# A layer norm applied to rows between two sets of transposes, in place of statistics sent through DRAM

## The chip, the cores and the metric

The kernel runs on one core of a Trainium2 chip. The metric is the device time of one execution in microseconds; a profiled execution gives the traces. The engines are TensorE (PE; PEld is its weight load), VectorE (DVE), ScalarE (ACT), GpSimd (POOL) and SyncE (SP), whose queue issues nearly all transfers between DRAM and the on-chip memory.

## The reference

One layer of a streaming encoder, for 2048 prompt tokens and 32 sample tokens (with 1024 cached). A combined projection of the normed input feeds two groups. The convolution group, which the change touches, has 512 channels; the attention group has 8 heads with a compressed key/value latent.

```python
h = _rmsnorm(x, g_pre)
a, b, gate_c, q_c, kv_c, k_r, gate_a = jnp.split(h @ w_in, SPLITS, axis=-1)
glu = a * jax.nn.sigmoid(b)
y = depthwise_conv(concat(hist, glu), width 31) + conv_b          # 512 channels
y_conv = silu(_layernorm(y, ln_g, ln_b))                          # over the 512 channels of a token
...                                                               # attention gives y_att
mixed = concat(y_conv * silu(gate_c), y_att * silu(gate_a)) @ w_out
return x + _rmsnorm(mixed, g_post)
```

`_layernorm` takes mean and variance of each token over its 512 channels, subtracts, divides, then applies a gain and a bias for each channel.

## The kernel before, in words

The work runs in three stages. **Stage A** makes the projection in two halves of 1024 tokens (the second with the 32 sample tokens), with channels on the partitions and tokens in the columns: for each block of 128 channels, TensorE multiplies each of two or three token chunks by the weight, each product as three matmuls of a high and a low part (lines 359 to 361). `load_w` loads a block's weight (512 KB through SP into one raw buffer); ScalarE rounds it to the high part, GpSimd subtracts for the low part (`split`, lines 155 and 156). Tokens come in as rows, are normed, and turned by TensorE (`transpose_x`, lines 330 to 332: ScalarE makes `xh`, VectorE makes `xl`). The order within a half is a and b blocks (GLU), latents, then the gates; in half 0 the last two gate blocks (`lastpair`) run with the loading of half 1's tokens among them.

The convolution is **background work**: `later(f, cost)` puts closures into a queue, and `bg(n)`, called behind each chunk of matmuls, takes from it what `n` pays for. 31 taps for each of four channel blocks run on VectorE into PSUM (line 381) and on ScalarE and GpSimd into `acc` (lines 386 to 390). In half 0 the layer norm follows in the same queue. What `bg` puts out stands in program order; a scheduler at build time then orders each engine's instructions by a timeline that it simulates.

The layer norm of a tile of 128 tokens: `emit_ln` turns the four blocks of `acc` into a PSUM tile with tokens on the partitions (line 198); VectorE takes mean and variance of each row (lines 178 and 179); GpSimd makes the inverse root with an add and a power (lines 142 and 143); SP writes the 128 pairs to DRAM (`st_d`, line 185) and reads them back as a row that is broadcast to all partitions (`z`, line 187); two places later in the queue `emit_ln2` subtracts and multiplies `acc` by these rows on VectorE (line 193). When all tiles are done, `emit_mix` takes one channel block with all its 1024 tokens: it loads the gate (line 206), applies gain, bias and Silu on ScalarE (line 208), multiplies on GpSimd, stores to `mix_d` (line 210).

**Stage B** is the attention. Here the order of TensorE, ScalarE, VectorE and GpSimd is written by a planner in the kernel: streams of steps (`q`, `s`, `t`, `v`, `p`, `l`, `o`) and a list of loose steps (`after`) are put out in order of simulated times, with a price for each step (`hold`, `t_pe`, `t_act`, `t_dve`; a transfer counts `DL` = 10 us). Keys and values are made, copied by ScalarE into one of four staging buffers (`staged`, line 834; two of them are halves of the tile `lng`), stored to DRAM, and loaded again for each head. The layer norm of half 1's nine tiles is stream `l`, one tile for every `BI` = 4 steps: `l_run` turns, `stats` sends the statistics through DRAM, `norm` subtracts and multiplies on GpSimd 20 simulated us later and stores the rows unscaled to `mix_d` (line 1403). Gain, bias, Silu and gate for them follow in **stage C**, the output projection (`split_mix`, line 1683).

SP's queue issues in order: a transfer that waits for a semaphore holds those behind it.

## Time and profile before

| | |
|---|---|
| median of 3 runs | 1310.7 us (1310.13 to 1317.46) |
| the profiled execution | 1310.61 us, span 1308.8 us |
| TensorE busy | 1232.9 us, 94% of the span |
| VectorE, ScalarE, GpSimd busy | 883.0 (67%), 749.2 (57%), 627.2 us (48%) |
| mean granted clock of TensorE | 0.974 of full speed |

A row of a busy table gives for each engine the time in which it had work in that stretch. The granted clock is TensorE's, 1.00 at 2.4 GHz and 0.50 at 1.2 GHz; between them, both occurred. "Idle before" is the time an engine stood still just before the instructions of a group, with the instruction or transfer that ended it.

### The profile page before, as it was taken

The page shows a single profiled execution, that of the slowest core. Times are in us where ns is not written, and L with a number is a line of the kernel's source. Part 1 is how long each engine was busy: PE and PEld are TensorE (multiplying, and loading weights), DVE is VectorE, ACT ScalarE, POOL GpSimd, SP SyncE. Part 2 cuts the span into 40 slices and gives each one's busy share as a digit, 9 for nine tenths or more (in the row PEclk, how much of TensorE's full clock was granted, in tenths as well). Part 3 has the DMA queues.
Part 4 walks back from the last instruction along what each step waited for, and adds up shares of the span by engine and source line. Part 5 has one row for each costly group of instructions (what it writes and reads, how often), then busy time and mean ns, then how long its engine had stood idle before and what let it go on. Part 6 is the DMA issues. An engine that isn't in the chain of part 4 may idle for free.

```text
span 1308.8 us, 20918 instructions
## 1 busy us (share of the span) xinstructions
PE 1232.9 (94%) x7272; PEld 1100.1 (84%) x7272; DVE 883.0 (67%) x1814; ACT 749.2 (57%) x1748; POOL 627.2 (48%) x680
## 2 busy tenths in 40 slices
PE   7999999699999998868996999999999999999997
PEld 6889987589899997757896999999999998788876
DVE  4299898255997913646684888898988884543333
ACT  5366722155565223656685888888888884345221
POOL 5299942136999322545554434545554365111110
PEclk8999999899899999989998999999999999999999
DMA  8122253223313323596666323355245356944332
GB/s 294 31 72 80 79 140 105 56 57 109 113 49 87 113 83 91 107 117 123 115 76 92 37 44 43 76 58 63 46 79 47 39 90 132 284 156 144 95 109 69
DMA packets 166606, 124.23 MB, mean 95 GB/s; under 512 B 67031, under 2 KB 148489, under 8 KB 166499
## 3 DMA queue, kind: packets, MB, share of 16 engines
q1 hardware_dynamic: 166339, 122.82, 42.2%
q8 instruction: 57, 0.93, 0.4%
q14 instruction: 50, 0.41, 0.3%
q10 hardware_dynamic: 160, 0.07, 0.0%
HBM read 83.64 MB, written 39.21 MB: 94 GB/s over the span
## 4 chain that ended last, share of the span: by engine, by line
PE 71%; DMA 13%; DVE 6%; POOL 5%; ACT 3%; issue 2%; SPq 1%; POOLq 0%; DVEq 0%; ACTq 0%
PE mm L361 7%; PE mm L360 7%; PE mm L359 7%; PE sps L1117 4%; PE sps L1119 4%; PE sps L1118 4%; DMA st_d<-bmv 3%; PE ops L1255 2%; PE yx L1710 2%; PE yx L1711 2%; PE yx L1709 2%; DVE cv L381 2%; PE sps L1711 2%; PE sps L1710 2%; PE sps L1709 2%; PE mm L441 2%
## 5 line engine op out<-in xcount | busy, mean ns | idle before, releaser
L381 DVE SCALAR_TENSOR_TENSOR cv<-glu,cwT,cv 128x1024 f32<-128x1024 f32 x186 | 239.7, 1289 | 6.0
L1154 ACT ACTIVATE pc<-pc,row 128x512 f32<-128x512 f32 (+3 forms) x320 | 210.2, 659 | 34.3 <-DVE pc L1133 33.6
L360 PE MATMUL mm<-xl,wh 128*128 128x352 f32 (+1 forms) x584 | 209.2, 358 | 2.6 <-DVE xl L347 2.5
L361 PE MATMUL mm<-xh,wl 128*128 128x352 f32 (+1 forms) x584 | 208.0, 356 | 3.2 <-POOL wl L156 3.2
L359 PE MATMUL mm<-xh,wh 128*128 128x352 f32 (+1 forms) x584 | 208.0, 358 | 0.3 <-ACT xh L331 0.3
L1224 DVE TENSOR_TENSOR ptl<-tp,pth 128x512 fp32r<-128x512 f32 (+1 forms) x288 | 187.8, 656 | 28.9 <-ACT pth L1220 26.2
L1220 ACT CAST pth<-tp 128x512 fp32r<-128x512 f32 (+1 forms) x288 | 159.9, 558 | 35.0 <-PE tp L1208 24.7
L1133 DVE TENSOR_SCALAR_CACHE_REDUCE pc<-sps,row 128x512 f32<-128x512 f32 (+2 forms) x192 | 125.7, 655 | 21.8 <-PE sps L1119 14.6
L1117 PE MATMUL sps<-kh,qh 128*128 128x512 f32 (+3 forms) x320 | 132.8, 415 | 4.0 <-DVE pc L1133 2.6
L360 PEld LDWEIGHTS mm<-xl,wh 128*128 128x128 f32 x584 | 112.2, 192 | 13.8 <-DVE xl L347 3.9
L361 PEld LDWEIGHTS mm<-xh,wl 128*128 128x128 f32 x584 | 112.3, 192 | 13.3 <-POOL wl L156 3.5
L1119 PE MATMUL sps<-kh,ql 128*128 128x512 f32 (+3 forms) x320 | 116.7, 365 | 6.6 <-POOL ql L156 6.6
L359 PEld LDWEIGHTS mm<-xh,wh 128*128 128x128 f32 x584 | 112.4, 193 | 10.9 <-ACT xh L331 0.6
L149 POOL TENSOR_TENSOR acc<-acc,ptap 128x512 f32<-128x512 f32 x92 | 118.7, 1306 | 4.6 <-ACT acc L386 2.7
L1118 PE MATMUL sps<-kl,qh 128*128 128x512 f32 (+3 forms) x320 | 116.1, 363 | 0.0
L156 POOL TENSOR_TENSOR wl<-wraw,wh 128x1024 fp32r<-128x1024 f32 x27 | 64.9, 2403 | 97.6 <-ACT wh L155 97.5
L156 POOL TENSOR_TENSOR ql<-qf,qh 128x256 fp32r<-128x256 f32 x64 | 46.9, 735 | 114.0 <-ACT qh L155 98.8
L1255 PE MATMUL ops<-ptl,vb 128*128 128x256 f32 x288 | 85.9, 298 | 5.6 <-DVE rl L1163 4.4
L1253 PE MATMUL ops<-pth,vb 128*128 128x256 f32 x288 | 88.2, 306 | 2.2 <-ACT pth L1220 2.2
L149 POOL TENSOR_TENSOR yp<-yp,low 64x256 f32<-64x256 f32 x64 | 46.9, 734 | 89.2 <-ACT low L1264 88.1
L1133 DVE TENSOR_SCALAR_CACHE_REDUCE pc<-sps 128x512 f32<-128x512 f32 (+3 forms) x128 | 80.0, 628 | 12.8 <-PE sps L1119 11.2
L1202 PE MATMUL tp<-ident,pc 128*128 128x128 f32 x288 | 80.3, 279 | 6.6 <-ACT lng L834 4.9
(386 smaller groups left out, 3265.2 us busy)
## 6 DMA issues: line engine op xcount, KB each, us to landing
wraw<-in_w_in SPq DMA_DIRECT2D x31, 512.0 KB
xr<-in_x_prompt SPq DMA_DIRECT2D x16, 512.0 KB
out_y_p<-src SPq DMA_DIRECT2D x32, 256.0 KB
mix<-mix_d SPq DMA_DIRECT2D x7, 1024.0 KB
gate_d<-gt SPq DMA_DIRECT2D x24, 176.0 KB
xt<-in_x_prompt SPq DMA_DIRECT2D x8, 512.0 KB
gate_d<-gt SPq DMA_DIRECT2D x16, 256.0 KB
gat<-gate_d SPq DMA_DIRECT2D x32, 128.0 KB
```

The source lines that it names most:

```text
L149: nc.gpsimd.tensor_tensor(dst, x, y, op)
L359: nc.tensor.matmul(ps[:, :n], wh[:, k], rh, start=(k == 0), stop=False)
L360: nc.tensor.matmul(ps[:, :n], wh[:, k], rl, start=False, stop=False)
L361: nc.tensor.matmul(ps[:, :n], wl[:, k], rh, start=False, stop=(k == KT - 1))
L381: nc.vector.scalar_tensor_tensor(box["ps"], x, cw(j), box["ps"], ALU.mult, ALU.add)
L1117: nc.tensor.matmul(d, qh[:, qs], kh[b][:, ks], start=True, stop=False)
L1118: nc.tensor.matmul(d, qh[:, qs], kl[b][:, ks], start=False, stop=False)
L1119: nc.tensor.matmul(d, ql[:, qs], kh[b][:, ks], start=False, stop=True)
L1133: nc.vector.tensor_scalar(p_[:, :m], d, -SCALE, r["mx"][:, c - 1:c] if c else None, ALU.mult, ALU.min, accum_out=r["mx"][:, c:c + 1])
L1154: nc.scalar.activation(p_, p_, AF.Exp, bias=r["mx"][:, ns - 1:ns], scale=-1.0, accum_out=r["ls"][:, c:c + 1])
L1220: nc.scalar.copy(out=ph[:, :nn], in_=ps[:, :nn])
L1224: nc.vector.tensor_tensor(pl[:, :nn], ps[:, :nn], ph[:, :nn].bitcast(F32), ALU.subtract)
```

## The change

The statistics no longer go through DRAM. VectorE applies mean and inverse root to the turned rows, where they are one number for each partition, and writes the normed rows into the place in `acc` that the tile's channels had; a second set of four transposes turns them back into PSUM (`ln_back`). In half 0, `emit_ln2` then applies gain, bias and Silu from PSUM to `acc` (four instructions for each tile), multiplies by the gate and stores to `mix_d`, tile by tile. The gate of a tile is loaded by `emit_ln` into one of two slots of the tile `lng`, which is now allocated once. `emit_mix` goes. The layer norm is queued after the convolution gates are made, and `emit_ln2` of a tile is queued ahead of `emit_ln` of the tile two later. Half 1's x transposes of `lastpair` take PSUM from the pool `mm` (four buffers) in place of `tp` (two). In stage B, `l_run` is followed by `stats` (with the tensor_scalar), `back` (transposes, in a further PSUM slot) and `out` (a copy by ScalarE, then the store). Two hunks that only name `lng` directly are left out here.

```diff
--- before.py
+++ after.py
@@ -162,52 +162,54 @@
     acc = accp.tile([P, CT, HALF + DEC], F32, name="acc")
 
     ln_pool = {}
-    zs = {}
+    lng = lnp.tile([P, HALF + DEC], F32, name="lng", bufs=1)
+    gslot = [lng[:, i * 512:(i + 1) * 512].rearrange("p (k t) -> p k t", k=CT) for i in range(2)]
 
     def queue_ln(jobs):
         for i in range(len(jobs) + LL):
+            if i >= LL:
+                later(lambda a=jobs[i - LL]: emit_ln2(*a), LC)
             if i < len(jobs):
                 later(lambda a=jobs[i]: emit_ln(*a), LC)
-            if i >= LL:
-                later(lambda a=jobs[i - LL]: emit_ln2(*a), LC)
-
-    def ln_stats(t, ps, r):
+
+    def ln_turn(ps, c0, r):
+        for i in range(CT):
+            nc.tensor.transpose(ps[:r, i * P:(i + 1) * P], acc[:, i, c0:c0 + r], ident)
+
+    def ln_rows(ps, c0, r):
 
         st = small.tile([P, 6], F32, name="bst")
         mv = small.tile([P, 2], F32, name="bmv")
         nc.vector.bn_stats(st[:r], ps[:r])
         nc.vector.bn_aggr(mv[:r], st[:r])
         rsqrt_eps(mv[:r, 1:2], mv[:r, 1:2], 1)
-        return mv
-
-    def ln_spread(t, mv, r):
-        rows = st_d[t * P:t * P + r]
-        nc.sync.dma_start(out=rows, in_=mv[:r])
-        z = lnp.tile([P, P, 2], F32, name="z")
-        nc.sync.dma_start(out=z[:, :r], in_=rows.partition_broadcast(P))
-        return z
-
-    def ln_apply(z, c0, r, subtract, multiply):
-        x = acc[:, :, c0:c0 + r]
-        for tt, op, q in ((subtract, ALU.subtract, 0), (multiply, ALU.mult, 1)):
-            tt(x, x, z[:, :r, q].unsqueeze(1).broadcast_to([P, CT, r]), op)
+        x = ln_x(c0, r)
+        nc.vector.tensor_scalar(x, ps[:r].rearrange("p (k c) -> p k c", k=CT), mv[:r, 0:1], mv[:r, 1:2],
+                                ALU.subtract, ALU.mult)
+
+    def ln_x(c0, r):
+        c0 = c0 if r == P else 0
+        return acc[:r, :, c0:c0 + P]
+
+    def ln_back(ps, c0, r):
+        x = ln_x(c0, r)
+        for i in range(CT):
+            nc.tensor.transpose(ps[:, i * P:i * P + r], x[:, i], ident[:r, :r])
 
     def emit_ln(t, c0, r):
         ps = ln_pool["ps"].tile([P, 512], F32, name="tp")
+        ln_turn(ps, c0, r)
+        ln_rows(ps, c0, r)
+        nc.sync.dma_start(out=gslot[t % 2], in_=gate_d[0:CT, :, c0:c0 + r].rearrange("k p t -> p k t"))
+
+    def emit_ln2(t, c0, r):
+        ps = ln_pool["ps"].tile([P, 512], F32, name="tp")
+        ln_back(ps, c0, r)
+        y = acc[:, :, c0:c0 + r]
         for i in range(CT):
-            nc.tensor.transpose(ps[:r, i * P:(i + 1) * P], acc[:, i, c0:c0 + r], ident)
-        zs[t] = ln_spread(t, ln_stats(t, ps, r), r)
-
-    def emit_ln2(t, c0, r):
-        ln_apply(zs.pop(t), c0, r, nc.vector.tensor_tensor, nc.vector.tensor_tensor)
-
-    def emit_mix(i, t0, n):
-        g = lnp.tile([P, HALF + DEC], F32, name="lng", bufs=1)
-        nc.sync.dma_start(out=g[:, :n], in_=gate_d[i, :, t0:t0 + n])
-        y = acc[:, i, :n]
-        nc.scalar.activation(y, y, AF.Silu, bias=col(LN_B, i), scale=col(LN_G, i))
-        pool_tt(y, y, g[:, :n], ALU.mult)
-        nc.sync.dma_start(out=mix_d[i, :, t0:t0 + n], in_=y)
+            nc.scalar.activation(y[:, i], ps[:, i * P:i * P + r], AF.Silu, bias=col(LN_B, i), scale=col(LN_G, i))
+        pool_tt(y, y, gslot[t % 2], ALU.mult)
+        nc.sync.dma_start(out=mix_d[0:CT, :, c0:c0 + r].rearrange("k p t -> p k t"), in_=y)
 
     with ExitStack() as pa:
         tp = pa.enter_context(tc.tile_pool(name="tpa", bufs=2, space=PSUM))
@@ -583,8 +585,6 @@
                             load_lat(lat_todo.pop(0))
                     bg(BG[half] / len(chunks))
                 conv_taps(i, half)
-            if half == 0:
-                queue_ln([(j, j * P, P) for j in range(8)])
             latents(half, tiles)
             if half:
                 def new_conv(dst, src, off):
@@ -608,8 +608,7 @@
                     evac_gate(half, slot, c0, m, emit_chunk(wts[key], c0, m))
                     bg(BG[half] / len(chunks))
                 if half == 0 and n == CT - 1:
-                    for i in range(CT):
-                        later(lambda i=i: emit_mix(i, 0, HALF), LC)
+                    queue_ln([(j, j * P, P) for j in range(8)])
             if lastpair:
                 need(lastpair[1])
                 owed[0] = 0.0
@@ -625,7 +624,7 @@
                             stage_x([ahead.pop(0)], 0)
                         bg(2 * LC)
                     if ci == 0:
-                        transpose_x(range(8, 12), 0, fill=True)
+                        transpose_x(range(8, 12), 0, mm, fill=True)
                 flush()
             if half:
                 bg(1e6)
...
@@ -1369,43 +1367,46 @@
             prods.pop(0)[2][1](ready)
 
 
-        zslots = Slots(4)
-        zslots.free = [0.0, 4.0, 12.0, 14.0]
         lns = list(ln_jobs)
         n_ln, n_done = [0], [0]
 
         def l_ready():
             if not lns or turn_at[0] < BS + BI * n_ln[0]:
                 return None
-            return latest(tps.ready(), zslots.ready())
+            return tps.ready()
 
         def l_run(ready):
             t, c0, r = lns.pop(0)
             n_ln[0] += 1
             kslot = tps.take()
             ps = tp.tile([P, 512], F32, name="tp")
-            for i in range(CT):
-                nc.tensor.transpose(ps[:r, i * P:(i + 1) * P], acc[:, i, c0:c0 + r], ident)
+            ln_turn(ps, c0, r)
             te = hold("pe", t_pe(256, 4), ready)
-            zk = zslots.take()
 
             def stats(ready):
-                mv = ln_stats(t, ps, r)
-                te = hold("dve", t_dve(512) + 0.1, ready)
+                ln_rows(ps, c0, r)
+                te = hold("dve", t_dve(512) + 0.2, ready)
+                te = hold("pool", 0.3, te)
+                te = hold("dve", t_dve(512), te)
                 tps.give(kslot, te)
-                te = hold("pool", 0.3, te)
-                z = ln_spread(t, mv, r)
-
-                def norm(ready):
-                    ln_apply(z, c0, r, pool_tt, pool_tt)
-                    te = hold("pool", 2.4, ready)
-                    zslots.give(zk, te)
+                after("pe", PE_["l"], lambda: latest(te, tps.ready()), back)
+
+            def back(ready):
+                k = tps.take()
+                ps = tp.tile([P, 512], F32, name="tp")
+                ln_back(ps, c0, r)
+                te = hold("pe", t_pe(256, 4), ready)
+
+                def out(ready):
+                    nc.scalar.copy(out=acc[:, :, c0:c0 + r], in_=ps.rearrange("p (k t) -> p k t", k=CT)[:, :, 0:r])
+                    te = hold("act", t_act(512), ready)
+                    tps.give(k, te)
                     nc.sync.dma_start(out=mix_d[0:CT, :, HALF + c0:HALF + c0 + r].rearrange("k p t -> p k t"),
                                       in_=acc[:, :, c0:c0 + r])
                     n_done[0] += 1
                     if n_done[0] == len(ln_jobs):
                         done["mix"] = te
-                after("pool", PE_["ln"], te + 2 * DL, norm)
+                after("act", PE_["ln"], te, out)
             after("dve", PE_["ln"], te, stats)
 
         pinned = ExitStack()
```

## Rows read from the trace of the kernel before

**Rows 1.** The page: TensorE's busy tenths in 40 slices of the span.
```profile
PE   7999999699999998868996999999999999999997
```

**Rows 2.** Stretches: length, busy PE, PEld, DVE, ACT, POOL, clock, DMA, GB/s.
```profile
220.00:260.00 40.00, 28.29 (x113) 21.86 (x113) 11.17 (x20) 5.95 (x9) 7.69 (x12) 0.83 0.33 76
260.00:300.00 40.00, 36.39 (x235) 34.40 (x236) 19.38 (x39) 19.84 (x36) 13.23 (x17) 0.96 0.20 51
300.00:340.00 40.00, 36.14 (x209) 35.56 (x208) 30.08 (x25) 21.09 (x32) 32.29 (x23) 0.91 0.49 143
...
560.00:600.00 40.00, 29.26 (x168) 24.14 (x167) 20.09 (x56) 23.75 (x56) 16.59 (x28) 0.87 0.84 128
...
680.00:720.00 40.00, 29.41 (x191) 27.50 (x190) 22.87 (x70) 22.90 (x61) 15.82 (x17) 0.88 0.65 91
```

**Rows 3.** TensorE in order of time: start, duration, unit, line, operation.
```profile
223.40 0.63 PE L359 MATMUL mm<-xh,wh 128*128 128x512 f32 x1
223.82 0.63 PE L360 MATMUL mm<-xl,wh 128*128 128x512 f32 x1
...
226.62 0.60 PE L198 MATMUL tp<-ident,acc 128*128 128x128 f32 x4
226.98 0.47 PE L359 MATMUL mm<-xh,wh 128*128 128x512 f32 x1
227.29 0.39 PE L360 MATMUL mm<-xl,wh 128*128 128x512 f32 x1
227.52 0.39 PE L359 MATMUL mm<-xh,wh 128*128 128x512 f32 x1
```

**Rows 4.** Groups, TensorE, 216 to 348 us: busy, ns | idle before, releaser.
```profile
L361 PE MATMUL mm<-xh,wl 128*128 128x352 f32 x115 | 38.9, 340 | 3.2 <-POOL wl L156 3.2
...
L330 PE MATMUL tp<-ident,xt 128*128 128x128 f32 x32 | 5.5, 299 | 11.1 <-DVE xl L332 5.6 <-DVE bst L178 5.4
L198 PE MATMUL tp<-ident,acc 128*128 128x128 f32 x32 | 5.0, 274 | 1.9 <-DVE acc L408 1.9
```

**Rows 5.** Groups of the other engines in 216 to 348 us.
```profile
L193 DVE TENSOR_TENSOR acc<-acc,z 128x512 f32<-128x512 f32 x16 | 11.0, 690 | 42.0 <-DMA z<-st_d 41.9
...
L208 ACT ACTIVATE acc<-acc,cols 128x1024 f32<-128x1024 f32 x4 | 4.6, 1232 | 6.2 <-DVE acc L193 6.2
...
L484 ACT ACT_TABLE_LOAD x2 | 2.6, 1283 | 0.0
L346 ACT ACTIVATE xh<-mm,cols 128x32 fp32r<-128x32 f32 x8 | 2.3, 288 | 13.1 <-DVE xl L347 11.7 <-PE mm L343 1.4
...
L149 POOL TENSOR_TENSOR acc<-acc,lng 128x1024 f32<-128x1024 f32 x4 | 9.6, 2406 | 7.2 <-ACT acc L208 6.8 <-DMA lng<-gate_d 0.4
```

**Rows 6.** SP's waits, 216 to 345 us: total us, times, longest.
```profile
SPq L187 <- DMA st_d<-bmv: 28.5, 7, 6.7
SPq L210 <- POOL acc L149: 22.6, 4, 6.6
```

**Rows 7.** SP's waits, 505 to 720 us.
```profile
SPq L187 <- DMA st_d<-bmv: 45.1, 9, 8.1
```

**Rows 8.** SP's issues in order of time: start, us, line, transfer.
```profile
541.27 0.32 SPq L185 DMA_DIRECT2D st_d<-bmv  x1
...
552.00 0.32 SPq L187 DMA_DIRECT2D z<-st_d  x1
```

**Rows 9.** The chain of waits in 505 to 720 us: start, us, what.
```profile
555.08 14.73 DMA v_d<-lng
...
683.71 9.56 DMA gat<-gate_d
```

**Rows 10.** Groups of GpSimd in 505 to 720 us.
```profile
L149 POOL TENSOR_TENSOR acc<-acc,z 128x512 f32<-128x512 f32 x16 | 20.9, 1307 | 0.6
...
L143 POOL TENSOR_TENSOR bmv<-bmv,nhalf 128x1 f32<-128x1 f32 x8 | 4.6, 571 | 0.7
```

More of the change, by code (lines that the diff above doesn't have):

```diff
@@ L681, in load_wkv @@
         def load_wkv():
-            raw = lnp.tile([P, HALF + DEC], F32, name="lng", bufs=1)[:, 0:NH * P].rearrange("p (h c) -> p h c", h=NH)
+            raw = lng[:, 0:NH * P].rearrange("p (h c) -> p h c", h=NH)
             nc.sync.dma_start(out=raw, in_=w_kvb.rearrange("p (h c) -> p h c", h=NH))
@@ L821, in prep_tasks @@
                     (lambda: latest(box["t2"], tps.ready()), query(1))]
-        spare = lnp.tile([P, HALF + DEC], F32, name="lng", bufs=1)
         stgw = wk.tile([P, 1024], F32, name="stgw", bufs=1)
         stgs = [stgw[:, i * 512:(i + 1) * 512] for i in range(2)]
-        stgs += [spare[:, i * 512:(i + 1) * 512] for i in range(2)]
+        stgs += [lng[:, i * 512:(i + 1) * 512] for i in range(2)]
         stg = Slots(len(stgs))
```

## The prediction

> **What bounds the kernel now.** I read the summary first: of 40 slices of 32.7 us, TensorE is busy for nine tenths or more in all but the first and the last, one at 229 us and several between 490 and 720 us [rows 1], so a change can only pay where TensorE stands still, runs at its lower clock, or loses work. The table by stretches says how much that is [rows 2]. These are the two places of the layer norm: its first half is worked off in the background around the turn from half 0 to half 1, its second half inside the attention plan.
>
> In 220 to 340 us TensorE idles 11.7 + 3.6 + 3.9 = 19.2 us. The granted clock of 0.83, 0.96 and 0.91 means that 34%, 8% and 18% of these stretches ran at 1.2 instead of 2.4 GHz; weighted with the busy share that is 19 us of work. A 512-column matmul follows the one before it after 0.42 us at the lower clock and 0.23 us at the upper [rows 3], so 45% of 19 us, 8.6 us, is lost. Together **28 us are lost in this stretch**.
>
> What ends these waits? The transposes of x wait 11.1 us for VectorE (for the split of x and for the statistics), others 1.9 us for the last convolution tap, and one matmul 3.2 us for GpSimd's weight split [rows 4]. VectorE itself is not busy then: its 16 subtract and multiply instructions stood 41.9 us waiting for the broadcast statistics [rows 5]. The split and the statistics stood behind them in its queue, and TensorE behind those. The SP queue is held too: before each broadcast it waits until the write of the statistics has landed, 28.5 us in seven times [rows 6], and weight loads stand behind that. So the round trip through DRAM is on the path here.
>
> In the attention stage the same wait holds SP for 45.1 us in nine times [rows 7]. The two worst stretches lose 10.7 and 10.6 us idle [rows 2], and by the same sum as above 3.4 and 3.2 us to the clock: **28 us** in both. The first is tied to the round trip: SP issues a statistics write at 541.3 us and its broadcast only at 552.0 us [rows 8]; behind it go the stores of k and v, of which the one issued at 555.1 us takes 14.7 us, and ScalarE's next evacuation, then TensorE, wait for its staging buffer [rows 9]. In the second the chain runs through a gate load of 9.6 us [rows 9] for which GpSimd waits with the key split behind it; SP was late there for several reasons, one of them a broadcast.
>
> After 720 us nothing of the layer norm is left, so what TensorE gains or loses before is passed on to the end.
>
> **The change part by part: half 0.** It removes 8 statistics writes, 8 broadcasts and the 16 VectorE instructions (11.0 us of work, 41.9 us of waiting [rows 5]). It adds on VectorE 8 tensor_scalar of 512 columns out of PSUM, 8 x 0.69 = 5.5 us by the nearest row [rows 5]. They wait for GpSimd's add and power; the power takes 0.57 us [rows 10]. Behind that wait on VectorE stand the split of x and the next statistics, for about 1 us a tile, 8 us in place of 41.9.
>
> TensorE gets 8 x 4 transposes back. Four of them cost 0.36 + 0.31 - 0.23 = 0.44 us of its time [rows 3], so 3.5 us. They come two places of the background queue after the first four; in between a whole chunk of 24 matmuls, 5.6 us, runs, which covers the chain from statistics to tensor_scalar (about 3 us). If that cover were gone, 8 x 3 us would stand on TensorE.
>
> ScalarE's 4 Silu of 1024 columns (1.23 us) become 32 of 128 columns. Between 0.29 us for 32 columns and 1.23 us for 1024 [rows 5] a straight line gives an estimate of 0.38 us, 12.2 us for 4.9. The last five tiles fall among half 1's sigmoids; if each comes alone, I count 9 table loads where 3 are now, 6 x 1.28 = 7.7 us more [rows 5]. ScalarE is busy for 26 of 80 us in 220 to 300 us [rows 2], so I cost both at nothing; if all of the table loads stood before an evacuation that TensorE waits for, it would be 8 us.
>
> On this a rule of the Trainium skill speaks against the change. The loads here last 1.28 us, and the sigmoid starts right behind one. The page "ScalarE: Activation LUTs", section "What ACT_TABLE_LOAD costs", adds a drain of about 1.38 us to that, 2.66 us a switch, and asks that calls be batched by table set. By the page the six would cost ScalarE 16 us; the trace shows only the 1.28 us of it.
>
> GpSimd's gate multiplication goes from 4 x 2.41 = 9.6 us [rows 5] to 8 x 1.31 = 10.5 us [rows 10], but most of it moves ahead of 300 us, where it is 74% idle [rows 2], and out of 300 to 340 us, where it is busy for 32 of 40 us and delays the weight split that TensorE waits for (3.2 us [rows 4], and the lower clock after it). The x transposes move to the larger PSUM pool, so that they no longer share two buffers with the layer norm; that goes with the waits above. Half 1's convolution overwrites the accumulator and waits for the last tile's store, as it now waits for the four stores of channels.
>
> SP: 8 gate loads of 256 KB replace 4 of 512 KB, 8 stores replace 4. A gate load writes over the slot of two tiles before, so SP waits for that tile's multiplication first; the store of that tile waits for the same thing. The nearest row is the 22.6 us that SP waits for 4 multiplications before their stores [rows 6], 5.6 us each. Behind them stand the weight loads, of which the first two of half 1 have little slack. No row shows the new order; the bounds are 0 (the wait falls where nothing is due) and 5.6 us for each of 8 tiles; I take 5 us on TensorE for this and all other new waits, near the low end, since the multiplication is then no longer behind a broadcast.
>
> Sum of half 0: of 28 us, 4 us stay (the wait for the last tap with the lower clock after it), 3.5 us of transposes and 5 us of new waits are added: **15.5 us gained**, between 5 (new waits of 15 us) and 24 (none, and the transposes inside waits).
>
> **Half 1, in the attention plan.** 9 statistics writes and 9 broadcasts go, with SP's 45.1 us of waiting; GpSimd loses 20.9 us of work for the eight full tiles [rows 10]. TensorE gets 9 x 0.44 = 4 us, VectorE 9 x 0.69 = 6.2 us, ScalarE 9 copies of 512 columns, about half of a 1.23 us row, 5.5 us. VectorE's new wait for GpSimd is planned at 0.3 us where the power alone takes 0.57 [rows 10]; attention's score evacuations stand behind it, some 9 x 0.7 us on an engine that is half idle in these stretches [rows 2]. The plan's order changes too, as its costs do. Of the 14 us of the first stretch I take 8 as gained, because the stores stood directly behind the blocked queue; of the 14 us of the second a quarter, because SP had other waits there; the added 4 us on TensorE are paid in full. **7.5 us gained**, between 4 lost and 24 gained.
>
> **Sum.** The profiled execution took 1310.6 us (span 1308.8), the median of three is 1310.7, so the two are the same: 1310.6 - 15.5 - 7.5 = **1288 us**.
>
> **The rivals.** (a) *Only half 0 gains.* k and v still go through four staging buffers, and the stores themselves are slow (14.7 us [rows 9]); then the attention stage stands as before, with about 2 of its added 4 us on the path: 1310.6 - 15.5 + 2 = 1297 us. For it speaks that those stores are on the chain; against it, that they were issued late. (b) *ScalarE takes back half 0's gain.* Five blocks of two table loads and four Silu (2 x 1.28 + 4 x 0.38 = 4.1 us) stand between sigmoid evacuations, and the weight chain behind them slips by most of 2.6 us for each: 13 us back, half 0 keeps 2.5, attention gives 2: 1310.6 - 2.5 - 2 = 1306 us. Against it speaks ScalarE's idle time. By the skill's price of a switch (same page and section) it would be twice that. (c) *Slower: SP is held longer than now.* If the gate loads of six tiles and the stores of eight each hold SP 5.6 us, that is 79 us against 28.5 + 22.6 = 51 us now [rows 6]. At today's rate (28 us lost for 51 held) TensorE loses 43 us, 15 more than now, with the transposes 1310.6 + 15 + 3.5 + 4 = 1333 us without a gain in attention, 1322 with it; about 1326. It decides when the mean wait goes over 51 / 14 = 3.6 us. Against it: the order is load and store behind the same multiplication, so that the second finds it done. (d) *SP wholly freed.* Both stretches of the attention stage recover and half 0 gains its 21: 1310.6 - 20 - 20 = 1270 us.
>
> **How the numbers follow.** Forecast 0.45 (1278 to 1296), (a) 0.22, (b) 0.13, (c) 0.08, (d) 0.12. From 1268 to 1307 us some 8 in 10 lie: it takes in the forecast, (a), about half of (b), most of (d), and leaves (c) out. About 1% is what a measurement here can tell from no change; 1% faster is 1297.6 us. (a) straddles that: faster 0.45 + 0.12 + 0.12 = 0.69; same 0.10 + 0.13 = 0.23; slower 0.08.
>
> **What would show it.** In the changed kernel's table by stretches, 220 to 340 us should show TensorE idle under 8 us and half 1's work starting some 15 us sooner. VectorE's waits for a transfer should be gone from the list of waits, its wait for GpSimd's power at about 1 us a tile. SP's waits should show the multiplication in place of the statistics; over 3.6 us each would mean (c). Up to 9 table loads in half 1's first chunks, with TensorE waiting for evacuations, would mean (b). In the attention stage the k and v stores should be issued within 2 us of their copies; if the two stretches there still lose 25 us or more, (a). The prediction fails most easily at the attention plan, whose order I cannot see, and at the weight loads behind the per-tile transfers.

## The result, and the profile after

The changed kernel takes **1276.8 us** (median of 4, 1270.2 to 1280.3) where the kernel before takes 1310.95 us (median of 4, 1310.1 to 1317.5): a ratio of **0.972, interval 0.967 to 0.978**. Timed again on another chip it took 1279.3 us against 1323.2 us, ratio 0.969 (0.965 to 0.974). Chips differ by 1% for the kernel before, so kernels are compared below by their ratio to it on their own chip. One profiled execution below, that of the kernel far, was a disturbed one (1343 us, where its others took 1317 to 1326), with a single wait of 24.4 us that stands behind 340 us, so only what comes before is read. The profiled execution took 1270.2 us (span 1268.4), 40.4 us less than that of before.

The page's row of busy tenths no longer has the dip at 229 us, and in the slices round 555 and 680 us an 8 is left where there was a 6 [rows 1]:
```profile
PE   7999999999999998989998999999999999999998
```

The same stretches as in [rows 2], busy times and granted clock:
```profile
220.00:260.00 40.00, 36.98 (x212) 31.71 (x211) 19.91 (x32) 20.19 (x39) 16.79 (x20) 0.96 0.48 142
260.00:300.00 40.00, 39.39 (x255) 38.77 (x256) 23.27 (x32) 25.91 (x51) 23.55 (x23) 1.00 0.31 84
300.00:340.00 40.00, 40.00 (x253) 40.00 (x252) 38.82 (x31) 24.99 (x42) 38.63 (x32) 1.00 0.16 46
...
560.00:600.00 40.00, 37.34 (x236) 32.26 (x235) 26.87 (x69) 26.82 (x63) 14.25 (x24) 1.00 0.73 114
...
680.00:720.00 40.00, 38.20 (x272) 35.58 (x273) 36.34 (x116) 35.05 (x95) 15.95 (x20) 1.00 0.44 53
```
TensorE idles 3.0 + 0.6 + 0 = 3.6 us in 220 to 340 us, where it idled 19.2, and the clock is granted in full from 260 us on. The attention stretches idle 2.7 and 1.8 us instead of 10.7 and 10.6. The work has moved up by 21 us by then, though, so these two stretches don't hold the same work; experiment 1 compares the same work.

The groups of 216 to 348 us that answer to [rows 4] and [rows 5]:
```profile
L187 DVE TENSOR_SCALAR acc<-tp,bmv 128x512 f32<-128x512 f32 x8 | 6.5, 810 | 7.4 <-POOL bmv L143 7.2
L210 ACT ACTIVATE acc<-tp,cols 128x128 f32<-128x128 f32 x32 | 12.0, 463 | 4.0 <-PE tp L197 3.9
L486 ACT ACT_TABLE_LOAD x3 | 3.8, 1283 | 1.4 <-PE mm L363 1.3
L210 ACT ACT_TABLE_LOAD x2 | 2.6, 1283 | 0.0
L177 PE MATMUL tp<-ident,acc 128*128 128x128 f32 x32 | 5.5, 273 | 1.9 <-DVE acc L410 1.9
L197 PE MATMUL tp<-ident,acc 128*128 128x128 f32 x32 | 5.0, 272 | 0.0
L332 PE MATMUL mm<-ident,glu 128*128 128x128 f32 x32 | 4.5, 274 | 1.3 <-DVE xl L334 1.3
```
VectorE's 41.9 us of waiting for the broadcast have become 7.2 us for GpSimd's power. TensorE's waits are the last tap (1.9 us, as before) and 1.3 us for the split of x. The transposes back waited for nothing.

SP's waits, 200 to 345 us, and then 484 to 700 us (the longest rows of each):
```profile
SPq L255 <- POOL wl L156: 42.8, 7, 14.1
SPq L212 <- POOL acc L149: 28.3, 7, 14.9
SPq L497 <- ACT gt L496: 27.8, 7, 6.5
...
SPq L1289 <- DMA rl_d<-rl: 35.0, 6, 13.2
SPq L884 <- ACT stgw L832: 11.3, 6, 6.1
```
SP still stands a good deal, but the statistics are out of both lists. In the second it waits for ScalarE's copy before it stores v, where ScalarE used to wait for the store [rows 9]. Its longest row there is another round trip through DRAM (`rl`), which the change doesn't touch.

**Where the time came from.** Two marks in the trace cut it in two: the last evacuation of a gate on ScalarE (the projection's end) and the last pair of stores of the attention result. The first moved from 507.1 to 486.2 us, 20.9 us. The second moved from 1101.7 to 1062.1 us, 39.6 us, so attention gave 18.7 in this pair of executions; 0.8 us came after.

### The profile page after: what moved, and what is told of

It reads as the page before. It is cut to its first block, busy times and chain, and to the rows that moved or that the text cites. A ratio compares the mean times of both kernels' runs of the same rounds, so it can differ in the third digit from the quotient of the medians.

```text
span 1268.4 us, 21075 instructions
## 1 busy us (share of the span) xinstructions
PE 1226.2 (97%) x7340; PEld 1098.2 (87%) x7340; DVE 887.2 (70%) x1815; ACT 762.8 (60%) x1787; POOL 606.4 (48%) x666
## 4 chain that ended last, share of the span: by engine, by line
PE 81%; DMA 6%; DVE 6%; ACT 2%; POOL 2%; issue 2%; SPq 0%; POOLq 0%; DVEq 0%; ACTq 0%
PE mm L361 9%; PE mm L362 9%; PE mm L363 9%; PE sps L1115 4%; PE sps L1117 4%; PE sps L1116 4%; PE ops L1253 2%; DMA gat<-gate_d 2%; DVE cv L383 2%; PE ops L1251 2%; PE sps L1710 2%; PE yx L1711 2%; PE sps L1711 2%; PE yx L1710 2%; PE yx L1712 2%; PE sps L1712 2%
## 5 line engine op out<-in xcount | busy, mean ns | idle before, releaser
L1152 ACT ACTIVATE pc<-pc,row 128x512 f32<-128x512 f32 (+3 forms) x320 | 210.4, 659 | 37.9 <-DVE pc L1131 35.0
L362 PE MATMUL mm<-xl,wh 128*128 128x352 f32 (+1 forms) x584 | 205.6, 352 | 0.0
L363 PE MATMUL mm<-xh,wl 128*128 128x352 f32 (+1 forms) x584 | 204.3, 351 | 0.0
L1218 ACT CAST pth<-tp 128x512 fp32r<-128x512 f32 (+1 forms) x288 | 159.7, 557 | 28.3 <-PE tp L1206 21.7
L392 ACT ACTIVATE ptap<-glu,cwT 128x512 f32<-128x512 f32 x92 | 65.8, 723 | 36.7 <-POOL acc L149 36.3
```

The lines of the kernel that those rows point to most:

```text
L362: nc.tensor.matmul(ps[:, :n], wh[:, k], rl, start=False, stop=False)
L363: nc.tensor.matmul(ps[:, :n], wl[:, k], rh, start=False, stop=(k == KT - 1))
L1152: nc.scalar.activation(p_, p_, AF.Exp, bias=r["mx"][:, ns - 1:ns], scale=-1.0, accum_out=r["ls"][:, c:c + 1])
L1218: nc.scalar.copy(out=ph[:, :nn], in_=ps[:, :nn])
```

## The experiments

All twelve, with the ratio to the kernel before on the same chip. "Projection" is the first mark in the profiled execution, "attention" the way from the first to the second, both in us.

```
kernel            ratio (interval)         projection  attention
before            1                        507.1       594.7
changed           0.972 (0.967 to 0.978)   486.2       576.0
changed, again    0.969 (0.965 to 0.974)   486.2       585.0
half0_only        0.981 (0.978 to 0.985)   485.3       609.2
half1_only        0.987 (0.983 to 0.990)   508.3       591.8
held0             0.980 (0.974 to 0.985)   495.0       596.6
held1             0.989 (0.985 to 0.992)   483.5       617.7
far               0.999 (0.997 to 1.002)   -           -
pool_apply        1.004 (1.001 to 1.008)   516.4       612.2
z_late            1.001 (0.998 to 1.005)   508.7       610.0
z_later           0.996 (0.993 to 0.999)   504.6       605.9
pool_queue        0.997 (0.993 to 1.000)   504.7       592.8
mix_by_channel    0.966 (0.962 to 0.971)   485.7       589.6
back_four         0.977 (0.973 to 0.981)   493.7       594.6
```
The first two lines of attention are from a faster chip; on the others the old layer norm through SP gives 606 to 612 us there, and the changed kernel 9 us more than on the first. An attention figure of one execution is good to some 10 us: on one chip 25 executions of the kernel before lie between 1314 and 1333 us. The projection lies within about 4 us for kernels with the same half 0.

**1. Each half alone** (half0_only, half1_only). Two kernels that carry the new layer norm in one half and the old one in the other:
```
-                ln_rows(ps, c0, r)
+                mv = ln_stats(t, ps, r)
...
+                z = ln_spread(t, mv, r)
...
+                    ln_apply(z, c0, r, pool_tt, pool_tt)
```
```
-        ln_rows(ps, c0, r)
+        zs[t] = ln_spread(t, ln_stats(t, ps, r), r)
...
+        ln_apply(zs.pop(t), c0, r, nc.vector.tensor_tensor, nc.vector.tensor_tensor)
```
The first edit of the changed kernel is half0_only (the plan has the old layer norm again), the second half1_only (with emit_mix of the kernel before, too).

> The change in half 0 alone; the attention plan keeps statistics through DRAM. Theory (the two halves gain by themselves, half 0 because VectorE no longer stands behind the broadcast): the last projection matmul, which ended at 507 us before and at 486 us after, ends at 486 us again, and the run gains that 21 us: about 1290 us (1284 to 1295). Rival (half 0's gain only shows because half 1 gained too, or is given back in the attention stage by the held SP queue): 1300 us or more.

> The change in the attention plan alone; half 0 keeps statistics through DRAM and the gates by channel block. Theory: 220 to 340 us looks as before, the attention stage is shorter by the 18 us that the two profiles show (from the end of the projection to the last store of the attention rows 597 us before, 580 us after): about 1293 us (1288 to 1298). Rival (the attention stage gained only because it began at another point of the transfers' traffic): 1303 us or more.

Half 0 alone gains 1.9%, attention alone 1.3%. On the first chip, for which the expectations were written, these ratios make 1287 and 1293 us, both inside the range of the theory. The product of the two, 0.968, is the whole (0.969 and 0.972), so the halves add up and neither is an effect of the other. The two attention stretches stay much as they were with half 0 alone (first fence) and recover in part with attention alone (second):
```profile
560.00:600.00 40.00, 32.37 (x185) 27.41 (x184) 20.71 (x54) 22.45 (x53) 18.32 (x28) 0.92 0.72 104
680.00:720.00 40.00, 29.77 (x186) 27.88 (x187) 22.71 (x76) 22.84 (x60) 17.49 (x22) 0.83 0.48 66
```
```profile
560.00:600.00 40.00, 34.65 (x209) 28.54 (x208) 26.30 (x68) 28.40 (x68) 12.88 (x29) 1.00 0.58 139
680.00:720.00 40.00, 33.88 (x232) 32.31 (x232) 26.84 (x88) 26.80 (x71) 20.16 (x23) 0.87 0.42 86
```
A stretch at a fixed time holds other work in each kernel. The score matmuls of attention (`sps<-kh,qh` in the traces, 320 in each kernel) mark the same work; the us from the start of one to the start of another are
```
score matmul      17th to 33rd   33rd to 81st   81st to 89th   89th to 129th
before            50.2           88.0           29.5           61.3
half0_only        54.5           87.4           30.0           61.3
changed           42.1           87.8           19.8           61.3
changed, again    42.8           88.0           19.1           62.1
half1_only        43.5           88.9           22.1           61.3
held1             54.9           90.0           30.5           61.6
pool_queue        42.6           91.2           23.2           61.3
```
In the kernel before, the 17th to the 33rd are 558 to 608 us and the 81st to the 89th 696 to 726 us: the two stretches of the prediction. Attention's gain stands in these two places, 8 to 11 us in each; between and behind them the same work takes nearly the same time.

**2. SP held again, by unused round trips** (held0, held1). The changed kernel, in which the statistics are also written and broadcast as before, into a tile that nobody reads; in half 0, or in the attention plan.
```
+    def round_trip(t, mv, r):
+        rows = st_d[t * P:t * P + r]
+        nc.sync.dma_start(out=rows, in_=mv[:r])
+        z = lnp.tile([P, P, 2], F32, name="z")
+        nc.sync.dma_start(out=z[:, :r], in_=rows.partition_broadcast(P))
...
-        ln_rows(ps, c0, r)
+        round_trip(t, ln_rows(ps, c0, r), r)
```


> The changed kernel, and in half 0 SP also writes the statistics to DRAM and broadcasts them back into a tile that nobody reads: SP's queue is held as before, VectorE waits for no transfer. Theory (most of half 0's loss was VectorE's wait, the held queue the smaller part): 4 to 8 us slower than the changed kernel, the projection ends at 490 to 494 us. Rival (the held SP queue and the late weight loads were the loss): 15 to 21 us slower, end near 505 us. Second rival (the held queue cost nothing): under 2 us.

> The changed kernel, and in the attention plan SP also writes the statistics and broadcasts them into a tile that nobody reads. Theory (the attention stage gained because SP's queue is no longer held in front of the stores of k and v): most of the 18 us comes back, 10 to 18 us slower than the changed kernel, with ScalarE waiting for stores of k and v again. Rival (it gained because GpSimd was relieved of 21 us of subtracting and multiplying, or because the plan's order is another): under 4 us slower.

In half 0 SP stands 37.9 us for the writes (first line), and TensorE waits 6.1 us for the evacuation of a gate (second). The projection ends at 495.0 us, 8.8 us later, a little more than expected: of the 21 us that half 0 gained, the unused round trip takes some 9 back. By their ratios the whole kernels differ by 10 to 14 us, more than the 4 to 8 expected; in the traces the rest lies in attention, to which nothing was added (596.6 us for 585.0). Part of the writes' 37.9 us stands in the place of SP's waits for the multiplication, which fall from 28.3 to 5.7 us.
```profile
SPq L195 <- DMA st_d<-bmv: 37.9, 8, 6.9
...
PE mm L339 <- ACT gt L503: 6.1, 1, 6.1
```
In attention it takes everything back. SP stands 30.5 us, and ScalarE waits for stored staging buffers again, 14 us where the changed kernel has none (2.1 us when traced again); the stretch at 680 us idles 12.5 us at a clock of 0.83. The ratio rises from 0.969 to 0.989, more than attention alone had gained, and both places of experiment 1 are as long as with the old layer norm (54.9 and 30.5 us).
```profile
SPq L195 <- DMA st_d<-bmv: 30.5, 8, 5.8
...
ACT lng L839 <- DMA k_d<-lng: 7.6, 2, 5.7
ACT stgw L839 <- DMA k_d<-stgw: 6.5, 2, 6.0
```
```profile
680.00:720.00 40.00, 27.51 (x172) 25.77 (x173) 20.90 (x72) 20.78 (x57) 16.73 (x22) 0.83 0.49 70
```
So unused round trips are enough to lose attention's gain, and GpSimd's relief or the plan's new order doesn't save it. They hold SP, but their transfers also take time on the DMA engines, and this run doesn't part the two. That a held SP is all that attention had lost doesn't follow; 4 asks that.

**3. Half 0: distance, or another engine to wait** (far, pool_apply). The kernel before with one more place between statistics and subtract; and with subtract and multiply on GpSimd.
```
-LL = 2
+LL = 3
...
-        ln_apply(zs.pop(t), c0, r, nc.vector.tensor_tensor, nc.vector.tensor_tensor)
+        ln_apply(zs.pop(t), c0, r, pool_tt, pool_tt)
```


> The kernel before, with subtract and multiply of half 0 put three places of the background queue behind the statistics instead of two. My theory: in half 0 both queues in which the broadcast's round trip is waited for matter, VectorE's with the split of x behind it and SP's with the weight loads behind it. One place is a chunk of 5.6 us, which is about the mean wait of a tile's subtract (42 us over 8 tiles, 5.2 us each), so VectorE's wait should fall from 42 to under 15 us, TensorE's idle time in 220 to 340 us from 19 to 10 or 13 us, and the time by 6 to 12 us (ratio 0.991 to 0.995); SP is held as before (28 us). Rival, the gain of half 0 needs the way through DRAM to go, distance can't help because each round trip starts later too: VectorE's wait stays over 30 us and the ratio lies between 0.997 and 1.003.

> The kernel before, with subtract and multiply of half 0 on GpSimd instead of VectorE; the statistics still go through DRAM and SP is still held 28 us. My theory: VectorE's 42 us of waiting held the split of x and the statistics, and through them TensorE; SP's share is what the unused round trip beside the new layer norm gave back, 9 us of the 21. Then VectorE has no waits for a transfer, and what is lost moves to GpSimd, where only the weight split stands behind it, with more slack: TensorE's idle time in 220 to 300 us falls from 15 to 6 or 9 us, the time by 5 to 12 us (ratio 0.991 to 0.996). Rival, the weight split on GpSimd is as tight as the split of x: TensorE waits for weights instead, idle time stays at 15 us or more and the ratio is 1.000 to 1.010.

My theory failed for pool_apply; far misses its aim and tests no theory. Its VectorE waits 40.0 us (41.9 before), but the distance didn't grow: from 222 to 276 us VectorE does the same seven statistics and the subtracts of the same four tiles, in the order of the kernel before. Only the eighth tile's statistics come earlier, ahead of the sixth tile's subtract and no longer behind the seventh's. The places of the queue give the program order; the build's scheduler ordered the engines nearly as it had. VectorE of the kernel before, then of far:
```profile
242.99 1.42 DVE L193 TENSOR_TENSOR acc<-acc,z 128x512 f32<-128x512 f32 x2 [4.89 <-DMA z<-st_d]
244.33 0.69 DVE L178 BATCH_NORM_STATS2 bst<-tp 128x6 f32<-128x512 f32 x1
248.94 0.69 DVE L193 TENSOR_TENSOR acc<-acc,z 128x512 f32<-128x512 f32 x1 [3.92 <-DMA z<-st_d]
```
```profile
242.05 1.42 DVE L193 TENSOR_TENSOR acc<-acc,z 128x512 f32<-128x512 f32 x2 [5.22 <-DMA z<-st_d]
243.39 0.69 DVE L178 BATCH_NORM_STATS2 bst<-tp 128x6 f32<-128x512 f32 x1
248.50 0.69 DVE L193 TENSOR_TENSOR acc<-acc,z 128x512 f32<-128x512 f32 x1 [4.42 <-DMA z<-st_d]
```
What the trace of far does show, as that of before would, is how the round trips stand in line on SP:
```profile
231.36 0.38 SPq L185 DMA_DIRECT2D st_d<-bmv  x1
238.73 0.32 SPq L187 DMA_DIRECT2D z<-st_d  x1
239.16 0.37 SPq L185 DMA_DIRECT2D st_d<-bmv  x1
243.79 0.32 SPq L187 DMA_DIRECT2D z<-st_d  x1
```
Each broadcast waits for its write, 7.4 and 4.6 us here, and the next write comes behind the broadcast. If that limits how many round trips pass in a time, more distance alone wouldn't help; no run shows it.

On GpSimd the wait is no cheaper: VectorE no longer waits for a transfer, but GpSimd does, for 35.6 us, and the weight split stands behind its subtracts. TensorE waits 17.9 us for the split (3.2 us before [rows 4]) and idles 20.6 us in 220 to 300 us, where my theory had 6 to 9. The profiled execution, the longest of ten, ends the projection 9 us later; the ratio of 1.004 is 5 us.
```profile
L361 PE MATMUL mm<-xh,wl 128*128 128x352 f32 (+1 forms) x144 | 51.5, 357 | 17.9 <-POOL wl L156 17.9
```

**4. Attention: SP freed, the rest as before** (z_late, z_later, pool_queue). The broadcast as a step of its own in the plan, 1.5 and then 4 planned transfer times after the write; last, both transfers issued by GpSimd.
```
-                z = ln_spread(t, mv, r)
+                rows = st_d[t * P:t * P + r]
+                nc.sync.dma_start(out=rows, in_=mv[:r])
...
+                def spread(ready):
+                    box["z"] = lnp.tile([P, P, 2], F32, name="z")
+                    nc.sync.dma_start(out=box["z"][:, :r], in_=rows.partition_broadcast(P))
+                    hold("sp", 0.4, ready)
...
-                after("pool", PE_["ln"], te + 2 * DL, norm)
+                after("sp", PE_["gate"], te + 1.5 * DL, spread)
+                after("pool", PE_["ln"], te + 2.5 * DL, norm)
```
This is z_late. z_later has 4 and 5.5 in the last two lines. pool_queue has nc.gpsimd for nc.sync, "pool" for "sp", and 1.5 and 3.

> The kernel before, in whose attention plan the broadcast of the statistics is a step of its own, due 1.5 transfer times after the write, so that SP issues other transfers in between instead of waiting; statistics still go through DRAM, GpSimd still subtracts and multiplies, no transposes are added. My theory: what the attention stage lost was SP held in front of the stores of k and v. Then SP's waits for the statistics in 505 to 720 us fall from 45 to under 12 us, the stretches at 560 and 680 us recover, and the time falls by as much as with the new layer norm in the attention plan alone or more, 14 to 20 us (ratio 0.985 to 0.990). Rival, the gain came from GpSimd's 21 us of relief or from the plan's new order: the ratio is 0.996 or more, with SP's wait gone and the stretches as slow as before.

> The same as the broadcast at 1.5 transfer times, but due 4 transfer times (40 us of the plan) after the write, with subtract and multiply at 5.5. With 1.5 the manipulation failed: SP still waited 37.8 us in eight times for the write, so that run tells nothing of a freed SP. My theory, SP held in front of the stores of k and v is what the attention stage lost: SP's waits for the statistics fall below 12 us, the stretches round 560 and 700 us lose some 15 us less, and the ratio is 0.985 to 0.992. Rival, the waits for slow stores, GpSimd's subtract and multiply, or the plan's order are the loss: SP's waits fall as much and the ratio stays at 0.996 or more.

> The kernel before, in whose attention plan both transfers of the statistics are issued by GpSimd instead of SP, the broadcast a step of its own 1.5 transfer times after the write, subtract and multiply 3 after it. In the two kernels with a late broadcast on SP's queue the traces still show it one to four entries behind its write and SP waiting 38 and 50 us, because SP's order is not written out by the plan. GpSimd's order is, so that here some 10 to 20 of its instructions stand between the two and nobody should be held. Statistics still go through DRAM, GpSimd still does the 21 us of subtracting and multiplying, and nothing is transposed back. My theory, the attention stage lost its time because SP stood in front of the stores of k and v: SP's waits for the statistics are gone, ScalarE's waits for stored staging buffers fall from 21 us to under 6, and the time falls by what the new layer norm gained in the attention plan alone, or most of it, 12 to 20 us (ratio 0.985 to 0.991). Rival one, GpSimd's work or the transfers themselves are the loss: SP's waits are gone and the ratio is still 0.996 or more. Rival two, GpSimd's queue is held in SP's place (its own waits for the write over 20 us): the ratio is 1.000 or more and GpSimd's key and value splits wait.

The first two miss their aim, and tell nothing of a freed queue: SP still waits 37.8 and 49.7 us. In the trace of z_later only one entry stands between this write and its broadcast, although 40 us of the plan do:
```profile
578.97 2.35 SPq L1398 DMA_DIRECT2D st_d<-bmv  x1
581.41 0.53 SPq L911 DMA_DIRECT2D src<-k_d  x1
586.64 0.32 SPq L1403 DMA_DIRECT2D z<-st_d  x1
587.05 0.38 SPq L860 DMA_DIRECT2D k_d<-stgw  x1
```
The plan pins the order of TensorE, ScalarE, VectorE and GpSimd only (its manual_schedule names these four); SP's order is not its own.

On GpSimd's queue the aim is met. SP's waits for the statistics are gone, GpSimd waits for none of the writes, and ScalarE's waits for stored staging buffers fall from 20.7 to 5.4 us. Yet the time falls by only 0.35% (0.03 to 0.66), where the new layer norm gains 1.3%; z_later, with SP held longer than before, measures as much (0.39%). GpSimd's rows of 505 to 720 us show what is left and what I added:
```profile
L149 POOL TENSOR_TENSOR acc<-acc,z 128x512 f32<-128x512 f32 (+1 forms) x18 | 21.8, 1214 | 2.0 <-DMA z<-st_d 1.2
...
L1398 POOL DMA_DIRECT2D st_d<-bmv x9 | 5.8, 649 | 2.7 <-POOL bmv L143 2.4 <-issue 0.3
L1403 POOL DMA_DIRECT2D z<-st_d x9 | 5.2, 578 | 0.0
```
```profile
577.61 2.70 POOL L149 TENSOR_TENSOR acc<-acc,z 128x512 f32<-128x512 f32 x2
...
583.64 2.67 POOL L149 TENSOR_TENSOR acc<-acc,z 128x512 f32<-128x512 f32 x2
586.27 1.44 POOL L156 TENSOR_TENSOR ql<-qf,qh 128x256 fp32r<-128x256 f32 x2
```
Issuing 18 transfers costs GpSimd 11 us, and its subtract and multiply stand in front of the split of q (586.3 us) on the chain of waits. The one trace says more for SP than the twelve runs do: in the table of experiment 1 both places are nearly as short as with the new layer norm (42.6 and 23.2 us), with 3 us more between them. But it is of the shortest of the twelve executions (1305.9 us, median 1316.9), and where the longer ones lose their 11 us no trace shows. **By the runs, freeing SP in this way brings a quarter of attention's gain; by its one trace, most of it.** Rival one stands by its ratio. How much of the rest is the old subtract and multiply, how much the new issues and how much the transfers themselves (3.7% of the DMA engines' time in 505 to 720 us, beside 56.9% for what SP issues) stays open.

**5. Per-token gates, and the transposes back** (mix_by_channel, back_four). The changed kernel with gates per channel block in half 0 as before; and with the transposes back made four times over.
```
-        for i in range(CT):
-            nc.scalar.activation(y[:, i], ps[:, i * P:i * P + r], AF.Silu, bias=col(LN_B, i), scale=col(LN_G, i))
-        pool_tt(y, y, gslot[t % 2], ALU.mult)
+        nc.scalar.copy(out=acc[:, :, c0:c0 + r], in_=ps.rearrange("p (k t) -> p k t", k=CT))
...
+                    for i in range(CT):
+                        later(lambda i=i: emit_mix(i, 0, HALF), LC)
```
```
-        ln_back(ps, c0, r)
+        for _ in range(4):
+            ln_back(ps, c0, r)
```


> The changed kernel with the gates of half 0 per channel block again, as before: ScalarE copies the rows transposed back to the accumulator (8 copies of 512 columns), and four Silu, four multiplications of 1024 columns and four stores follow at the end. My theory: per-token gates carry the part of half 0's gain that has to do with GpSimd in 300 to 340 us, the 3.2 us wait for the weight split and the lower clock behind it, about 6 of the 21 us; TensorE idles 3 to 6 us more in 300 to 340 us and the ratio to the kernel before is some 0.004 higher than the changed kernel's 0.969. Rival, per-token gates are a cost (32 Silu of 0.46 us, two table loads more, SP waiting for each multiplication) that the layer norm pays for: then this kernel is as fast as the changed one or 2 to 5 us faster, a ratio of 0.965 to 0.969.

> The changed kernel with the transposes back in half 0 made four times over (96 transposes more; the last result is used). My price of 0.44 us for four, worked out from matmul spacing, gives 24 x 0.44 = 10.6 us in full: the projection ends 10 or 11 us later than in the changed kernel (496 or 497 us instead of 486), the ratio is 0.977 instead of 0.969, and the changed kernel's own eight groups cost it 3.5 us. Rival, they run inside waits of TensorE that are there anyway: under 4 us, a ratio of 0.969 to 0.972. A second rival, the fourth group delays Silu and with it the gates that half 1 needs: over 15 us, 0.981 or more.

Gates per token are worth nothing that can be measured: without them the ratio is 0.966 (0.962 to 0.971), the projection ends at 485.7 us, and 300 to 340 us is full although GpSimd is busy for 39.5 us of it:
```profile
300.00:340.00 40.00, 40.00 (x253) 40.00 (x252) 29.08 (x24) 22.30 (x38) 39.50 (x31) 1.00 0.41 125
```
Four times the transposes cost 7.5 us at the projection's end (493.7 against 486.2), 0.31 us for four where I had 0.44. That is one execution of each, and the projection of kernels with the same new half 0 varies by some 3 us, so 0.2 to 0.4 us. The ratio of 0.977 is the expected one by luck: the rest of it lies in attention, where nothing was added.

## Why the prediction was right, and where its sizes were off

**Half 0: 15.5 us forecast, 20.9 measured.** The mechanism was the one named, the round trip through DRAM, with VectorE and SP both held by it: round trips that hold only SP take 9 us back (held0), and the subtract's wait, put on GpSimd, costs no less there (pool_apply). The other 12 us are VectorE's by subtraction only. No run parts them from two other things that the change moves, the place of the layer norm in the queue and the x transposes' larger PSUM pool. In pool_apply these transposes keep the two old buffers and wait 0.1 us where they waited 11.1 [rows 4], which speaks for VectorE's wait, though TensorE stands for weights there. The sum goes wrong in two terms. *New waits, 5 us*: what TensorE newly waits for is 1.7 us at most (3.6 us idle less the last tap's 1.9), and VectorE's wait for the power, 7.2 us in eight tiles for the 8 forecast, reaches TensorE hardly at all. *Transposes, 3.5 us*: about 2.5 at 0.31. With the clock of 0.96 in the first stretch, by the working of the prediction 0.08 x 37 x 0.45 = 1.3 us, 28 - 3.6 - 1.3 - 2.5 = 20.6 us.

**Costs on other engines.** tensor_scalar out of PSUM takes 0.81 us, not 0.69, and Silu of 128 columns 0.463, not 0.38. There are 5 table loads, not 9: several tiles' Silu came one behind the other. None of it stands among TensorE's waits, so costing ScalarE at nothing held and rival (b) fell. The page "ScalarE: Activation LUTs" of the Trainium skill, section "What ACT_TABLE_LOAD costs", adds a drain to each switch of the table set; the trace of the changed kernel shows the load's 1.28 us alone, with Silu beginning 0.02 us behind it:
```profile
274.71 0.28 ACT L348 ACTIVATE xh<-mm,cols 128x32 fp32r<-128x32 f32 x1
275.01 1.28 ACT L210 ACT_TABLE_LOAD   x1
276.31 1.50 ACT L210 ACTIVATE acc<-tp,cols 128x128 f32<-128x128 f32 x4
```

**Rival (c) and its point of decision.** SP waited 28.3 us in seven times for the multiplication, 4.0 us each, over the 3.6 us at which I said (c) would decide. It didn't come. The 3.6 us were 51 us shared among 14 waits, of six loads and eight stores; but only seven stores waited for a multiplication and no load did, as I had argued against (c), so the sum stayed at 28.3 us, under 51. "At today's rate" failed too: by it 28.3 us held would lose 15.5, and TensorE's new waits in 220 to 340 us are 1.7 us at most. mix_by_channel can't test this, for SP waits 26.2 us in four times for the multiplications there. In held0 SP's waits for the writes and the multiplication sum to 43.6 us, and the projection ends 9 us later than with the 28.3. I take it that what counts is what stands behind the waiting entry and when it is due; no run varies that alone.

**The weight split.** I laid TensorE's 3.2 us wait for it, and the lower clock after it, to GpSimd's multiplications in 300 to 340 us. mix_by_channel puts these back and the wait does not return, so that reason was wrong; what in the change removed the wait isn't shown.

**Attention: 7.5 us forecast, 13 to 19 measured** (1.3% of 1323 is 17 us; the medians of the first chip leave 34 - 21 = 13, the two executions 18.7). The direction and the first place were right: stores of k and v behind a held SP, which held1 brings back, and rival (a) fell. By the table of experiment 1 that place is 8.1 us shorter, for the 8 forecast. The step that failed is "of the 14 us of the second a quarter", 3.5 us: the 81st to the 89th score matmul take 9.7 us less (7.9 in half1_only against half0_only, on one chip), and held1 takes that back. I counted SP's other waits there as independent of the statistics; that the place recovers, and is lost again in held1, speaks against it, but which transfer carries the delay isn't shown. "The added 4 us on TensorE are paid in full" failed too: the gains of the two places have the transposes in them, and outside of them nothing was lost (87.8 us for 88.0, 61.3 for 61.3). So 8.1 + 9.7 = 17.8 us stand where I had 8 + 3.5 - 4. Whether a held SP is the whole cause stays open, as pool_queue shows; I had given GpSimd's 20.9 us [rows 10] no price at all.

The forecast's two short terms have the same sign, which is why the median came out 11 us below it and near rival (d). The sizes of (d), 20 us for each half, are nearly those of the two executions (20.9 and 18.7), though SP was not wholly freed: it still waits 28.3 us for the multiplication and 35.0 us for `rl`. That (d) had only 0.12 was part of the same mis-sizing.

## What to carry to other kernels

A round trip through DRAM whose second transfer waits on the queue that issues it costs that queue the landing of every write (28.5 us in half 0 here, 45.1 in attention). Giving the waiting step to another engine moved the wait there and gained nothing. Whether more distance would help was not shown: far, which was meant to add it, was built with nearly the old order, and in z_late and z_later the broadcast still stood close behind its write on SP. Before you price a held queue, list what stands behind the held entry and when each is due: 28 us of waiting cost TensorE under 2 us here in one place, and unused round trips that held SP for 30 us cost 2% in another. When a plan is to be tested by moving a step, see in the trace that the step moved, on the engine that was meant. And compare stretches by the work in them, not by the clock on the wall: at fixed times the second stretch seemed to lose nearly all of its idle time with both halves and less than half of it with attention alone.

## What the runs showed that I had not expected

- The same write of the statistics holds SP for 4.1 us on average in half 0 (28.5 us in seven [rows 6]) and 5.0 us in attention [rows 7], up to 11.9 us in z_later. The Trainium skill, page "DMA: Bandwidth & Descriptors", section "Anatomy of one DMA — SWDGE (gpsimd) path", says that a wait for a semaphore takes place at the engine that issues and not in the DMA engines; SP's rows agree (the 28.5 and 45.1 us are waits in SP's own queue). The fixed cost of about 2.0 us that the section gives for a transfer issued by GpSimd is less than half of what SP waited for these writes.
- A transfer issued by GpSimd takes 0.65 and 0.58 us of that engine's time (pool_queue), one issued by SP 0.32 us of SP's.
- The attention stage of the same changed kernel differs by 9 us between two chips, one execution on each, while the projection ends at the same time (486.2 us). The score matmuls up to the 129th take 211.1 and 212.0 us from the 17th on, so the difference comes behind them.
